# First MLP product as seven half-size block products, the weights' block sums added by GpSimd

## Chip, core and metric

The kernel runs on one core of a Trainium2 chip. The metric is the device time of one execution in microseconds (us). Of a core's engines, TensorE (PE in the profile, PEld for its weight loads) multiplies matrices into PSUM, VectorE (DVE) and ScalarE (ACT) work element by element on SBUF and PSUM, GpSimd (POOL) does so on SBUF, and SyncE (SP) issues the transfers from memory.

## What is computed

A two-layer decoder trunk on 256 tokens of width 2048, all in float32. Each layer is an attention mixer followed by an MLP whose hidden width is 8192; a norm ends it. The change is in the MLP alone:

```python
def sq_relu_mlp(h, w_up, w_down):
    u = jax.nn.relu(h @ w_up)      # (256 x 2048) @ (2048 x 8192)
    return (u * u) @ w_down        # (256 x 8192) @ (8192 x 2048)

# in reference(), for each layer i:
h = h + mixer(rmsnorm(h, norm[i]), ...)
h = h + sq_relu_mlp(rmsnorm(h, mlp_norm[i]), w_up[i], w_down[i])
```

## The kernel before

Tokens are two tiles of 128 (`NT`), the width 2048 is 16 chunks of 128 rows (`KC`), and one PSUM bank holds 512 columns (`HALF`). TensorE multiplies in float32r, so every operand is held as a sum hi + lo of two shorter numbers and a product is made of three: hi·hi, hi·lo and lo·hi. `split` (L172 to L175) makes such a pair: ScalarE casts the source into hi (L174), VectorE subtracts hi from the source into lo (L175). A weight tile of 128 x 1024 is split in one such pair of instructions.

The hidden width is worked through in eight blocks e of 1024 columns. The order in `mlp` (L577) is up(0), up(1) of a block, then the next block's two ups, then `down(e - 1)`; so in the steady part one period is two calls of `up` and one of `down`.

- `up(f)` (L582) makes 512 columns of the first product, transposed. The weights stand still in TensorE and the 256 tokens stream past, hi and lo side by side: for each of 16 chunks and 4 groups of 128 columns, `mm_wide` (L182) issues one product of 512 columns (L185) and one of 256 (L189). `sum_halves` (L193) adds the two halves of a bank, L598 does the squared ReLU, and `split` stores the result, already transposed, as an operand of `down`.
- `down(e)` multiplies that block of 1024 hidden columns by 1024 rows of `w_down`, in two halves of 2 x 512 output columns, by `gemm` (L277): tokens stand still, the weights stream (L296), 8 chunks x 2 token tiles x 3 products x 2 banks, so 192 products of 512 columns. `residual` (L552) adds the result into `h`.

`project` (L557) is the attention's output projection ahead of each MLP; after each half of its columns `norm_transpose` (L210) transposes `h` (L219), applies the gain and splits (L224, L225) into `xm`, the MLP's input.

Weights come by transfers on SP's queue into `wraw`, three buffers of 1 MB; hi tiles (`whi`) have four buffers and lo tiles (`wlo`) three, so the splits run a little ahead of TensorE. PSUM has six banks for accumulators (`ps`) and two for side work (`ps2`, tiles named `side`). The order on each engine is set by a scheduler that works on a list by program order and its own estimates; each engine then runs its list strictly in turn, waiting for semaphores.

Of the kernel before, what the change touches and what calls it, by code (L numbers as in the profile page):

```python
# [17 lines left out]
P = 128  # L18
# [6 lines left out]
NKV = 4  # L25
# [27 lines left out]
ARRIVE = 2  # L53

# [9 lines left out]
def shape_constants():  # L64
    """Rotary tables and position masks; they depend on the shapes alone."""
# [24 lines left out]
def yoco_kernel(ctx: ExitStack, tc: tile.TileContext, x, a_w_in, a_w_out, w_kv, b_w_q, b_w_out, w_up, w_down,  # L90
# [8 lines left out]
    keep = ctx.enter_context(tc.tile_pool(name="keep", bufs=1))  # L99
    wk = ctx.enter_context(tc.tile_pool(name="wk", bufs=2))  # L100
    ps = ctx.enter_context(tc.tile_pool(name="ps", bufs=6, space=bass.MemoryType.PSUM))
    ps2 = ctx.enter_context(tc.tile_pool(name="ps2", bufs=2, space=bass.MemoryType.PSUM))

# [1 line left out]
    def b4(dt=F32):  # L105
        return wk.tile([P, 1024], dt, name="b4" + ("r" if dt == F32R else ""), tag="b4", bufs=4)

    def b3(dt=F32):
        return wk.tile([P, 768], dt, name="b3" + ("r" if dt == F32R else ""), tag="b3", bufs=4)
# [49 lines left out]
    def rope(v, heads, half, tok, idx):  # L159
        """v: [P, heads, hd] view of an SBUF tile, rotated in place."""  # L160
# [21 lines left out]
    def mm_wide(acc, w_hi, w_lo, xk, first, last):  # L182
        """Weights stationary: the first half of acc takes w_hi x_hi + w_lo x_hi, the second w_hi x_lo."""
# [23 lines left out]
    def new_xt():  # L207
        return xtp.tile([P, 4, 2, SEQ], F32R, name="xt")

    def norm_transpose(c4, which):  # L210
        """Chunks 4*c4..4*c4+3 of h, times gain, transposed and split, for each gain in `which`.
        The row's 1/rms is applied where the product comes out."""
# [15 lines left out]

    class Stats:
        """Mean square of the rows of h, and what follows from it."""  # L230
# [34 lines left out]
    def load_w(w, r0, nk, cols, width):  # L265
        """Rows r0.. of nk chunks, `width` columns at each of cols: [P, nk, len(cols) * width]."""
# [36 lines left out]
    def transposed_split(dst, srcs):  # L303
        """dst: [P, hi/lo, n, P] view; srcs: n [P, P] tiles."""
# [7 lines left out]
    # ================= layer 1: sparse attention =================  # L312
# [19 lines left out]
    def arrive(k):  # L332
        """x's next columns, ahead of the product that needs them."""
# [22 lines left out]
    kiT = keep.tile([P, 2, SEQ], F32R, name="kiT")  # L356
    wi = [keep.tile([P, IH], F32, name=f"wi{t}") for t in range(NT)]
    maskA = keep.tile([P, NT, SEQ], F32, name="maskA", tag="layer_mask")
# [3 lines left out]
    def evac_qi(t, s, acc):  # L362
        """Without 1/rms: a positive factor per query, which goes into the heads' weights."""
# [11 lines left out]
    def index_keys():  # L375
        """The indexer's keys and head weights: weights stationary, so the product comes out transposed."""
# [44 lines left out]
    def select(t):  # L421
        """maskA[t]: 0 at the keys that the indexer picks for each query, BIG elsewhere."""
# [38 lines left out]
    kT = keep.tile([P, 2, NKV, SEQ], F32R, name="kT")  # L461
    vv = [keep.tile([P, 2, KV_W], F32R, name=f"vv{t}") for t in range(NT)]
    rkv = []

    def evac_kv(t, s, acc):
        """Keys, rotated and times -SCALE, transposed; values."""
# [14 lines left out]
    def values(kvh, t, n, probs, oT):  # L481
        """probs(r, kb): [P, P] tiles of normalised probabilities of n heads; oT: [P, n, hi/lo, token]."""
# [74 lines left out]
    def project(oTs, w, gains_next, cut):  # L557
        """The first `cut` chunks of both column halves come first: the others' heads may still be at work."""
        st = Stats()
        sets = [[] for _ in gains_next]  # L560
# [3 lines left out]
        flush()  # L564
        for n in range(2):
            gemm(stat, range(cut, KC), w, 0, (n * GW, n * GW + HALF), residual(st, n))
            for c4 in (2 * n, 2 * n + 1):
                for i, xt in enumerate(norm_transpose(c4, gains_next)):
                    sets[i].append(xt)
        return st, sets  # L570

    st, (xm,) = project(oTs, a_w_out[0], [G_M0], CUT_A)

    # ================= squared-ReLU MLP =================
    NE = DFF // GW

    def mlp(i, xm, st_in, gains_next, final=None):  # L577
        """(relu(r * y))^2 = r^2 * relu(y)^2, so the square of 1/rms is applied after the second product."""
# [3 lines left out]
        def up(f):  # L582
            """Columns 512*f.. of the first product, transposed: two halves of a bank, summed on the way out."""
            acc = [ps.tile([P, HALF], F32, name="acc") for _ in range(4)]
            for k4 in range(0, KC, 4):
                raw = load_w(w_up[i], k4 * P, 4, (f * HALF,), HALF)
                for k2 in range(k4, k4 + 4, 2):
                    hi = wp.tile([P, GW], F32R, name="whi", bufs=4).rearrange("p (k c) -> p k c", k=2)
                    lo = wp.tile([P, GW], F32R, name="wlo").rearrange("p (k c) -> p k c", k=2)
                    split(hi, lo, raw[:, k2 - k4:k2 - k4 + 2])  # L590
                    for c in range(4):
                        cs = slice(c * P, (c + 1) * P)
                        for k in (k2, k2 + 1):
                            mm_wide(acc[c], hi[:, k - k2, cs], lo[:, k - k2, cs], xm[k // 4][:, k % 4], k == 0, k == KC - 1)
            ut = new_xt()
            for c in range(4):
                s, q = sum_halves(acc[c]), b1()
                nc.vector.scalar_tensor_tensor(q, s, 0.0, s, op0=ALU.max, op1=ALU.mult)  # L598
                split(ut[:, c, 0], ut[:, c, 1], q)
            us[f] = ut  # L600
# [25 lines left out]
    st, (xkv, xq) = mlp(0, xm, st, [G_KV, G_B])  # L626

# [197 lines left out]
```

## Times and profile before

| what | value |
|---|---|
| median of three runs | 2210.43 us (2209.86 to 2210.74) |
| span of the profiled execution, first to last instruction | 2208.0 us |
| TensorE busy | 2196.8 us, 99% |
| VectorE busy | 1413.6 us, 64% |
| ScalarE busy | 1053.3 us, 48% |
| GpSimd busy | 0.7 us, 6 instructions |
| weights and data moved | 405 MB, mean 184 GB/s |

The profile gives, for one execution, the busy time of each engine, the chain of work that ended last (followed back from the end), groups of instructions by line with their mean duration, and who waited for whom. A busy TensorE is not the same as a TensorE at its peak: products overlap in its pipeline, so the time of a product is best taken from a stretch of products back to back divided by their number. The profiled execution lies 2.4 us below the median of the runs; sums below are made against the 2208.0 us of the span.

### The profile page before, as it was taken

The numbers are of one execution on the slowest core, as the hardware profiler recorded it, in microseconds if no ns is written. First come the engines' busy times: TensorE is split into PE (matmuls) and PEld (weight loads), VectorE is DVE, ScalarE is ACT, GpSimd is POOL, SyncE is SP. The second block draws the span as 40 slices with busy tenths as digits, with TensorE's granted clock in tenths as the row PEclk, the third lists the DMA queues.
The fourth block names the chain that finished last, engine by engine and source line by source line (L and its number), as shares of the span: only waits on it lengthen the run. The fifth ranks groups of instructions, "written<-read, shape, count | busy, mean of one in ns | idle before, by whom it ended". The sixth has DMA issues, their size and how long they took to land.

```text
span 2208.0 us, 29489 instructions
## 1 busy us (share of the span) xinstructions
PE 2196.8 (99%) x11366; PEld 1863.8 (84%) x11366; DVE 1413.6 (64%) x2215; ACT 1053.3 (48%) x1500; POOL 0.7 (0%) x6
## 2 busy tenths in 40 slices
PE   9999999999999999999999999999999999999998
PEld 7788888888888888888888888888888888888886
DVE  5877765656565656567577777666665656565656
ACT  6445554444444434446455555445444434444443
POOL 0000000000000000000000000000000000000000
PEclk9999999999999999999999999999999999999999
DMA  8464456666666666665555454566666665666663
GB/s 305 153 191 136 162 172 191 191 186 193 189 188 193 187 188 192 185 198 180 168 163 164 159 158 150 184 190 191 191 191 191 191 190 191 187 193 190 187 193 138
DMA packets 180749, 405.17 MB, mean 184 GB/s; under 512 B 11008, under 2 KB 60288, under 8 KB 180608
## 3 DMA queue, kind: packets, MB, share of 16 engines
q1 hardware_dynamic: 179456, 401.25, 58.1%
q10 hardware_dynamic: 1152, 2.04, 0.3%
q8 instruction: 89, 1.46, 0.3%
q14 instruction: 52, 0.43, 0.1%
HBM read 401.15 MB, written 2.10 MB: 183 GB/s over the span
## 4 chain that ended last, share of the span: by engine, by line
PE 98%; DVE 1%; ACT 0%; DMA 0%; issue 0%; SPq 0%; DVEq 0%; ACTq 0%
PE acc L296 60%; PE acc L185 22%; PE acc L189 11%; PE side L307 1%; PE side L178 1%; PE side L180 1%; PE side L179 1%; PE side L219 1%; DVE b L439 0%; PE acc L179 0%; PE acc L178 0%; PE acc L180 0%; PE side L660 0%; DMA b<-in_xt_dram 0%; DVE wlo L175 0%; PE side L661 0%
## 5 line engine op out<-in xcount | busy, mean ns | idle before, releaser
L175 DVE TENSOR_TENSOR wlo<-wraw,whi 128x1024 fp32r<-128x1024 f32 (+2 forms) x781 | 919.3, 1177 | 656.8 <-PE acc L296 349.5
L174 ACT CAST whi<-wraw 128x1024 fp32r<-128x1024 f32 (+2 forms) x781 | 792.7, 1015 | 1017.8 <-PE acc L296 610.6
L296 PE MATMUL acc<-whi,xt 128*128 128x512 f32 x4160 | 1093.1, 378 | 0.7 <-ACT whi L174 0.7
L296 PEld LDWEIGHTS acc<-whi,xt 128*128 128x128 f32 x4160 | 741.0, 188 | 140.4 <-ACT whi L174 2.5
L185 PE MATMUL acc<-xt,whi 128*128 128x512 f32 (+1 forms) x2064 | 721.1, 398 | 0.0
L296 PE MATMUL acc<-wlo,xt 128*128 128x512 f32 (+1 forms) x2080 | 616.2, 377 | 0.1
L189 PE MATMUL acc<-xt,wlo 128*128 128x256 f32 (+1 forms) x2064 | 558.5, 281 | 0.0
L185 PEld LDWEIGHTS acc<-xt,whi 128*128 128x128 f32 (+1 forms) x2064 | 379.3, 188 | 84.6
L296 PEld LDWEIGHTS acc<-wlo,xt 128*128 128x128 f32 x2080 | 372.4, 188 | 72.8 <-DVE wlo L175 0.4
L189 PEld LDWEIGHTS acc<-xt,wlo 128*128 128x128 f32 (+1 forms) x2064 | 388.9, 188 | 11.6
L552 DVE SCALAR_TENSOR_TENSOR h<-acc,ri,h 128x512 f32<-128x512 f32 x127 | 88.1, 747 | 11.1 <-PE acc L296 9.2
L174 ACT CAST xt<-b 128x256 fp32r<-128x256 f32 x128 | 51.7, 404 | 31.3 <-DVE b L598 30.3
L196 ACT COPY b<-acc 128x256 f32<-128x256 f32 (+1 forms) x129 | 47.4, 368 | 33.0 <-DVE b L197 31.2
L175 DVE TENSOR_TENSOR xt<-b,xt 128x256 fp32r<-128x256 f32 x128 | 53.9, 421 | 8.5 <-ACT xt L174 8.5
L197 DVE TENSOR_TENSOR b<-acc,b 128x256 f32<-128x256 f32 (+1 forms) x129 | 54.5, 423 | 6.8 <-ACT b L196 3.4
L598 DVE SCALAR_TENSOR_TENSOR b<-b 128x256 f32<-128x256 f32 x128 | 54.0, 422 | 1.7
L307 PE MATMUL side<-ident,b 128*128 128x128 f32 x256 | 38.5, 273 | 0.4 <-DVE b L170 0.4
L307 PEld LDWEIGHTS side<-ident,b 128*128 128x128 f32 x256 | 30.8, 141 | 6.2 <-issue 1.1
L225 DVE SCALAR_TENSOR_TENSOR xt<-side,gT,xt 128x256 fp32r<-128x256 f32 x64 | 28.8, 480 | 7.8 <-ACT xt L224 7.4
L237 ACT ACTIVATE b<-h 128x512 f32<-128x512 f32 (+1 forms) x41 | 25.2, 616 | 17.6 <-DVE h L552 10.6
L224 ACT ACTIVATE xt<-side,gT 128x256 fp32r<-128x256 f32 x64 | 28.3, 473 | 7.4 <-DVE xt L225 4.4
L679 ACT ACTIVATE b<-b,nmb 128x768 f32<-128x768 f32 (+1 forms) x32 | 24.6, 770 | 7.0 <-DVE nmb L676 7.0
(154 smaller groups left out, 750.6 us busy)
## 6 DMA issues: line engine op xcount, KB each, us to landing
wraw<-in_w_up_dram SPq DMA_DIRECT2D x128, 1024.0 KB, 5.7
wraw<-in_w_down_dram SPq DMA_DIRECT2D x128, 1024.0 KB, 5.5
wraw<-in_b_w_q_dram SPq DMA_DIRECT2D x192, 256.0 KB, 3.1
wraw<-in_a_w_in_dram SPq DMA_DIRECT2D x31, 1024.0 KB, 5.3
wraw<-in_a_w_out_dram SPq DMA_DIRECT2D x16, 1024.0 KB, 5.5
wraw<-in_b_w_out_dram SPq DMA_DIRECT2D x16, 1024.0 KB, 5.5
wraw<-in_w_kv_dram SPq DMA_DIRECT2D x8, 1024.0 KB, 4.9
h<-in_x_dram SPq DMA_DIRECT2D x8, 256.0 KB, 8.6
```

The lines of the kernel that those rows point to most:

```text
L174: nc.scalar.copy(hi, src)
L175: nc.vector.tensor_tensor(lo, src, hi.bitcast(F32), op=ALU.subtract)
L185: nc.tensor.matmul(acc, w_hi, xk.rearrange("p a t -> p (a t)"), start=first, stop=last)
L189: nc.tensor.matmul(acc[:, :SEQ], w_lo, xk[:, 0], start=False, stop=False)
L196: nc.scalar.copy(part, acc[:, SEQ:])
L197: nc.vector.tensor_tensor(total, acc[:, :SEQ], part, op=ALU.add)
L224: nc.scalar.activation(xt[:, cc, 0, :], pt[:, j, :], AF.Copy, scale=g)
L225: nc.vector.scalar_tensor_tensor(xt[:, cc, 1, :], pt[:, j, :], g, xt[:, cc, 0, :].bitcast(F32), op0=ALU.mult, op1=ALU.subtract)
L296: nc.tensor.matmul(acc[t][i][:, :c1 - c0], stat(k, a, t), b[:, c0:c1], start=first and a == 0 and b is hi, stop=last and a == 1)
L307: nc.tensor.transpose(pt[:, j * P:(j + 1) * P], sr, ident)
L552: nc.vector.scalar_tensor_tensor(hh, acc, scale()[:, t:t + 1], hh, op0=ALU.mult, op1=ALU.add)
L598: nc.vector.scalar_tensor_tensor(q, s, 0.0, s, op0=ALU.max, op1=ALU.mult)
```

## The change

The first product of the MLP is done for all 1024 columns of a block at once, by Winograd's form of Strassen's scheme: the tokens are halved (two tiles of 128), the reduction is halved into two interleaved sets of chunks, and the 1024 columns are halved into 512 + 512. Seven block products q1 to q7 take the place of eight. Their left operands are seven forms of the normalised activations, made once for each layer; their right operands are the four weight blocks x, w, y, z and three kinds of sums of them. The reduction runs in four steps u; in each, GpSimd makes four sums in place: x + w, then that + y, then that + z, and w + y. Each of the 28 pairs (q, u) is a `task`: a transfer where the block is new, a sum where one is needed, a split, and six products of 512 columns with tokens standing still. `TASKS` sets the order. The seven results are combined by one ScalarE copy and seven VectorE sums; then ReLU and square on ScalarE and a transposition by TensorE, since the result is no longer transposed.

```diff
+BLOCKS = {"x": (0, 0), "w": (0, 1), "y": (1, 1), "z": (1, 0)}
+CHAINS = (("x", None), ("z", None), ("y", None), ("x", "z"), ("x", "w"), ("x", "y"), ("w", "y"))
+NU = 4
+def task_order(gap=3):
+    chains = [c for u in range(NU) for c in ([(0, u), (4, u), (5, u), (3, u)], [(2, u), (6, u)], [(1, u)])]
...
+    open_scope("keep", "att")
...
+    def add_forms(forms, c4, which):
...
+                    nc.scalar.activation(gx[:, cc, :], pt[:, j, :], AF.Copy, scale=g)
...
+        nc.vector.tensor_tensor(s1, a22, a21, op=ALU.subtract)
+        nc.vector.scalar_tensor_tensor(v, s1, -1.0, a11, op0=ALU.mult, op1=ALU.subtract)
+        nc.vector.tensor_tensor(s3, a11, a21, op=ALU.subtract)
+        nc.vector.scalar_tensor_tensor(s4, v, -1.0, a12, op0=ALU.mult, op1=ALU.subtract)
...
+        for f, src in zip(forms, (a11, a12, s4, a22, s1, v, s3)):
+            split(f[:, q, 0], f[:, q, 1], src)
...
+        open_scope("mlp")
+        forms = new_forms()
         for n in range(2):
             gemm(stat, range(cut, KC), w, 0, (n * GW, n * GW + HALF), residual(st, n))
+            add_forms(forms, 2 * n, gain_next)
...
-        def up(f):
-            acc = [ps.tile([P, HALF], F32, name="acc") for _ in range(4)]
...
-                            mm_wide(acc[c], hi[:, k - k2, cs], lo[:, k - k2, cs], xm[k // 4][:, k % 4], k == 0, k == KC - 1)
...
+        def up(e):
+            acc = [ps.tile([P, HALF], F32, name="acc") for _ in range(6)] + [side()]
...
+            def task(q, u):
+                key, other = CHAINS[q]
+                for n in (key, other):
+                    if n is not None and (n, u) not in held:
+                        if n in "xz":
+                            held[n, u] = wx()
+                        else:
+                            both = wp.tile([P, 2, GW], F32, name="wraw", bufs=3)
...
+                            nc.sync.dma_start(held[m, u], block(u, *BLOCKS[m]))
+                if other is not None:
+                    nc.gpsimd.tensor_tensor(held[key, u], held[key, u], held[other, u], op=ALU.add)
...
+                split(hi, lo, held[key, u])
+                for k in range(2):
+                    x = xm[q][:, 2 * u + k]
+                    mm3(acc[q], x[:, 0], x[:, 1], hi[:, k], lo[:, k], u == 0 and k == 0, u == NU - 1 and k == 1)
+            for q, u in TASKS:
+                task(q, u)
+            q1, q2, q3, q4, q5, q6, q7 = acc
+            c11, c12, c21, c22 = (b2() for _ in range(4))
+            nc.scalar.copy(c11, q1)
+            nc.vector.tensor_tensor(c12, q6, c11, op=ALU.add)
...
+                    nc.scalar.activation(c, c, AF.Relu, scale=-1.0 if f else 1.0)
+                    nc.scalar.activation(c, c, AF.Square)
+                    transposed_split(us[2 * e + f][:, :, :, t * P:(t + 1) * P].rearrange("p c a t -> p a c t"),
+                                     [c[:, j * P:(j + 1) * P] for j in range(4)])
...
         for e in range(NE):
-            up(2 * e)
-            up(2 * e + 1)
+            up(e)
             if e:
                 down(e - 1)
```

The blocks x and z have tiles of their own (`wx`, six buffers); w and y share a `wraw` buffer. The tiles of the attention and those of the MLP now lie in the same memory, one set at a time (`open_scope`). The change's line numbers differ from the profile's; in the fences below L685 is GpSimd's sum, L213 the subtraction of a split (L175 before), L631 the residual (L552 before), L698 to L704 the seven sums of results, and L384 the subtraction of a transposed split (L310 before).

GpSimd's list held nothing but the start of the program. In a steady period of the change it holds these rows for one call of `up` (the first eight of sixteen; `wx_3988` and `wx_4000` are block x of steps 0 and 1, `wraw_4012` and `wraw_4036` the pairs w, y of the same steps, `wx_4072` and `wx_4128` block z):

```order
L685 TENSOR_TENSOR wx_3988<-wx_3988,wraw_4012 128x1024
L685 TENSOR_TENSOR wraw_4012<-wraw_4012 128x1024
L685 TENSOR_TENSOR wx_4000<-wx_4000,wraw_4036 128x1024
L685 TENSOR_TENSOR wraw_4036<-wraw_4036 128x1024
L685 TENSOR_TENSOR wx_3988<-wx_3988,wraw_4012 128x1024
L685 TENSOR_TENSOR wx_4000<-wx_4000,wraw_4036 128x1024
L685 TENSOR_TENSOR wx_3988<-wx_3988,wx_4072 128x1024
L685 TENSOR_TENSOR wx_4000<-wx_4000,wx_4128 128x1024
```

All sixteen sums are new; the same tile `wx_3988` is written three times, each time after the split of its former content.

VectorE at the end of a `down` and the start of the next `up`, before:

```order
L175 TENSOR_TENSOR wlo_4003<-wraw_4000,whi_4002 128x1024
L175 TENSOR_TENSOR wlo_4023<-wraw_4000,whi_4022 128x1024
L552 SCALAR_TENSOR_TENSOR h0_2_81<-acc_3852,ri_2882,h0_2_81 128x512
L552 SCALAR_TENSOR_TENSOR h0_3_82<-acc_3853,ri_2882,h0_3_82 128x512
L552 SCALAR_TENSOR_TENSOR h1_2_85<-acc_3854,ri_2882,h1_2_85 128x512
L552 SCALAR_TENSOR_TENSOR h1_3_86<-acc_3855,ri_2882,h1_3_86 128x512
L175 TENSOR_TENSOR wlo_4045<-wraw_4042,whi_4044 128x1024
```

The same place in the change:

```order
L213 TENSOR_TENSOR wlo_3991<-wx_3988,whi_3990 128x1024
L213 TENSOR_TENSOR wlo_4003<-wx_4000,whi_4002 128x1024
L631 SCALAR_TENSOR_TENSOR h0_2_84<-acc_3837,ri_2925,h0_2_84 128x512
L631 SCALAR_TENSOR_TENSOR h0_3_85<-acc_3838,ri_2925,h0_3_85 128x512
L631 SCALAR_TENSOR_TENSOR h1_2_88<-acc_3839,ri_2925,h1_2_88 128x512
L631 SCALAR_TENSOR_TENSOR h1_3_89<-acc_3840,ri_2925,h1_3_89 128x512
L213 TENSOR_TENSOR wlo_4016<-wraw_4012,whi_4015 128x1024
L213 TENSOR_TENSOR wlo_4027<-wx_3988,whi_4026 128x1024
```

Two splits of the coming `up` stand ahead of the four residuals in both; behind them now stand 26 more of that `up` in a row, 16 of which read a tile that GpSimd has just written.

VectorE at the end of an `up`, before (two of the four result tiles of `up`, with splits of `down` between):

```order
L197 TENSOR_TENSOR b1_3693<-acc_3505,b1_3692 128x256
L175 TENSOR_TENSOR wlo_3765<-wraw_3746,whi_3764 128x1024
L598 SCALAR_TENSOR_TENSOR b1_3696<-b1_3693 128x256
L197 TENSOR_TENSOR b1_3701<-acc_3506,b1_3700 128x256
L175 TENSOR_TENSOR xt_3675<-b1_3696,xt_3675 128x256
L598 SCALAR_TENSOR_TENSOR b1_3704<-b1_3701 128x256
```

The same place in the change (`acc_3982` to `acc_3986` and `side_3987` are six of the seven results):

```order
L213 TENSOR_TENSOR wlo_4303<-wraw_4209,whi_4302 128x1024
L213 TENSOR_TENSOR wlo_4369<-wraw_4366,whi_4368 128x1024
L699 TENSOR_TENSOR b2_4312<-acc_3982,b2_4312 128x512
L213 TENSOR_TENSOR wlo_4385<-wraw_4366,whi_4384 128x1024
L700 TENSOR_TENSOR b2_4315<-side_3987,b2_4313 128x512
L213 TENSOR_TENSOR wlo_4403<-wraw_4400,whi_4402 128x1024
L701 TENSOR_TENSOR b2_4313<-acc_3985,b2_4313 128x512
L703 TENSOR_TENSOR b2_4314<-acc_3984,b2_4315 128x512
L702 TENSOR_TENSOR b2_4313<-acc_3983,b2_4313 128x512
L704 TENSOR_TENSOR b2_4315<-acc_3985,b2_4315 128x512
L384 TENSOR_TENSOR xt_4324<-side_4327,xt_4324 128x4x128
L213 TENSOR_TENSOR wlo_4419<-wraw_4400,whi_4418 128x1024
```

The last split of `up` is followed by three of `down`, with the sums of the results between and behind them.

## Rows read from the trace of the kernel before

**Rows 1.** Page: busy time by engine; GpSimd's and the clock's rows by slices.
```profile
PE 2196.8 (99%) x11366; PEld 1863.8 (84%) x11366; DVE 1413.6 (64%) x2215; ACT 1053.3 (48%) x1500; POOL 0.7 (0%) x6
...
POOL 0000000000000000000000000000000000000000
PEclk9999999999999999999999999999999999999999
```

**Rows 2.** Chain in time: start us, length us, what; products of `down`, and transpositions.
```profile
113.93 0.63 PE side L307 x4
...
162.71 0.88 PE side L307 x8
...
411.06 43.52 PE acc L296 x192
499.74 43.52 PE acc L296 x192
...
854.46 43.52 PE acc L296 x192
```

**Rows 3.** Stretches of two `up` and of one `down`: length, busy us by engine, clock.
```profile
core 0: us, PE busy (x) PEld busy (x) DVE busy (x) ACT busy (x) POOL busy (x), PEclk, DMA share, GB/s
454.58:499.74 45.16, 45.16 (x258) 39.19 (x257) 26.36 (x34) 20.56 (x27) 0.00 (x0) 1.00 0.61 184
411.06:454.58 43.52, 43.52 (x193) 36.03 (x193) 26.58 (x32) 18.33 (x21) 0.00 (x0) 1.00 0.63 195
```

**Rows 4.** VectorE in an `up`: start, length, what [idle before, releaser].
```profile
377.29 1.22 DVE L175 TENSOR_TENSOR wlo<-wraw,whi 128x1024 fp32r<-128x1024 f32 x1 [1.58 <-PE acc L189]
380.12 1.23 DVE L175 TENSOR_TENSOR wlo<-wraw,whi 128x1024 fp32r<-128x1024 f32 x1 [1.61 <-PE acc L189]
```

**Rows 5.** Groups by line and shape: count, busy us, mean ns, idle before.
```profile
L175 DVE TENSOR_TENSOR wlo<-wraw,whi 128x1024 fp32r<-128x1024 f32 x649 | 793.9, 1224 | 606.7 <-PE acc L296 314.1 <-PE acc L189 268.4 <-issue 15.6
...
L174 ACT CAST whi<-wraw 128x1024 fp32r<-128x1024 f32 x649 | 683.3, 1053 | 874.7 <-PE acc L296 506.4 <-PE acc L185 325.8 <-issue 33.9
...
L552 DVE SCALAR_TENSOR_TENSOR h<-acc,ri,h 128x512 f32<-128x512 f32 x127 | 88.1, 747 | 11.1 <-PE acc L296 9.2 <-PE acc L180 1.9
...
L175 DVE TENSOR_TENSOR xt<-b,xt 128x256 fp32r<-128x256 f32 x128 | 53.9, 421 | 8.5 <-ACT xt L174 8.5
...
L225 DVE SCALAR_TENSOR_TENSOR xt<-side,gT,xt 128x256 fp32r<-128x256 f32 x64 | 28.8, 480 | 7.8 <-ACT xt L224 7.4
L224 ACT ACTIVATE xt<-side,gT 128x256 fp32r<-128x256 f32 x64 | 28.3, 473 | 7.4 <-DVE xt L225 4.4 <-PE side L219 2.1
L237 ACT ACTIVATE b<-h 128x512 f32<-128x512 f32 x39 | 24.4, 627 | 13.2 <-DVE h L552 10.6 <-DVE h L550 2.4
L550 DVE TENSOR_TENSOR h<-acc,h 128x512 f32<-128x512 f32 x32 | 20.6, 684 | 1.6 <-PE acc L296 1.6
...
L310 DVE TENSOR_TENSOR b4r<-side,b4r 128x512 fp32r<-128x512 f32 x24 | 16.2, 688 | 8.6 <-ACT b4r L309 8.6
...
L309 ACT CAST b4r<-side 128x512 fp32r<-128x512 f32 x24 | 13.6, 585 | 2.6 <-PE side L307 2.6
```

**Rows 6.** The same view, GpSimd alone.
```profile
masks.py:199 POOL TENSOR_SCALAR_AFFINE_SELECT ident<-ident 128x128 f32<-128x128 f32 x1 | 0.3, 292 | 0.1
masks.py:197 POOL MEMSET ident<- 128x128 f32 x1 | 0.2, 204 | 0.3 <-POOLq L813 0.3
...
L813 POOL MEMSET const-float32-0.0<- 128x1 f32 x1 | 0.1, 98 | 0.2 <-issue 0.2
```

**Rows 7.** Transfers: issuer, count, KB each, median us from issue to landing.
```profile
wraw<-in_w_up_dram SPq DMA_DIRECT2D x128, 1024.0 KB, 5.7
```

More of the change, by code (lines that the diff above doesn't have):

```diff
@@ L53 @@
 ARRIVE = 2
+BLOCKS = {"x": (0, 0), "w": (0, 1), "y": (1, 1), "z": (1, 0)}
[3 more added lines that the diff above has]
+    chains = [c for u in range(NU) for c in ([(0, u), (4, u), (5, u), (3, u)], [(2, u), (6, u)], [(1, u)])]
+    place, out = {}, []
+    ahead = 1
+    while any(chains):
+        now = len(out)
+        low = min(c[0][1] for c in chains if c)
+        ready = [c for c in chains if c and c[0][1] <= low + ahead and now - place.get(id(c), -gap) >= gap]
+        if not ready:
+            ready = [c for c in chains if c and c[0][1] <= low + ahead]
+        best = min(ready, key=lambda c: (c[0][1] - len(c), c[0][1]))
+        place[id(best)] = now
+        out.append(best.pop(0))
+    return tuple(out)
+TASKS = task_order()
 Q_W = NH * HD
@@ L98, in yoco_kernel, with open_scope @@
     wp = ctx.enter_context(tc.tile_pool(name="wp", bufs=3))
-    keep = ctx.enter_context(tc.tile_pool(name="keep", bufs=1))
     wk = ctx.enter_context(tc.tile_pool(name="wk", bufs=2))
+    scope = [None]
+    pools = {}
+    def open_scope(*names):
+        if scope[0] is not None:
+            scope[0].close()
+        scope[0] = ExitStack()
+        pools.clear()
+        for n in names:
+            pools[n] = scope[0].enter_context(tc.tile_pool(name=n, bufs=1))
+    open_scope("keep", "att")
     ps = ctx.enter_context(tc.tile_pool(name="ps", bufs=6, space=bass.MemoryType.PSUM))
@@ L354, in yoco_kernel @@
     split_x(0, raw_x)
-    kiT = keep.tile([P, 2, SEQ], F32R, name="kiT")
-    wi = [keep.tile([P, IH], F32, name=f"wi{t}") for t in range(NT)]
-    maskA = keep.tile([P, NT, SEQ], F32, name="maskA", tag="layer_mask")
+    kiT = pools["keep"].tile([P, 2, SEQ], F32R, name="kiT")
+    wi = [pools["keep"].tile([P, IH], F32, name=f"wi{t}") for t in range(NT)]
+    maskA = pools["keep"].tile([P, NT, SEQ], F32, name="maskA", tag="layer_mask")
     qiT = [[None, None] for _ in range(NT)]
@@ L459, in yoco_kernel, with new_kv @@
     enqueue([(index_all(), n_index)], 20)
-    kT = keep.tile([P, 2, NKV, SEQ], F32R, name="kT")
-    vv = [keep.tile([P, 2, KV_W], F32R, name=f"vv{t}") for t in range(NT)]
-    rkv = []
+    kT, vv, rkv = None, [], []
+    def new_kv():
+        nonlocal kT
+        kT = pools["keep"].tile([P, 2, NKV, SEQ], F32R, name="kT")
+        vv[:] = [pools["keep"].tile([P, 2, KV_W], F32R, name=f"vv{t}") for t in range(NT)]
+    new_kv()
     def evac_kv(t, s, acc):
@@ L555, in residual, with project @@
         return evac
-    def project(oTs, w, gains_next, cut):
+    def project(oTs, w, gain_next, cut):
         st = Stats()
-        sets = [[] for _ in gains_next]
         stat = stat_of(oTs)
@@ L564, in project @@
         flush()
+        open_scope("mlp")
+        forms = new_forms()
         for n in range(2):
             gemm(stat, range(cut, KC), w, 0, (n * GW, n * GW + HALF), residual(st, n))
[L567 to L572, printed above, removed]
+            add_forms(forms, 2 * n, gain_next)
+        return st, forms
+    st, xm = project(oTs, a_w_out[0], G_M0, CUT_A)
     NE = DFF // GW
@@ L626, in yoco_kernel @@
     st, (xkv, xq) = mlp(0, xm, st, [G_KV, G_B])
-    mb = keep.tile([P, NG * 3 * P], F32, name="mb", tag="layer_mask")
+    open_scope("keep", "att")
+    new_kv()
+    mb = pools["keep"].tile([P, NG * 3 * P], F32, name="mb", tag="layer_mask")
     nc.scalar.dma_start(mb, c_maskb)
@@ L706, in yoco_kernel @@
             enqueue([(attend_b(kvh, t, qb[t], oTs[-1][:, pr * PAIR:(pr + 1) * PAIR]), steps_b(t)) for t in range(NT)], SPREAD_B)
-    st, (xm,) = project(oTs, b_w_out[0], [G_M1], CUT_B)
-    fg = [b2() for _ in range(4)]
-    for s in range(4):
-        nc.scalar.dma_start(fg[s], final_norm[s * HALF:(s + 1) * HALF].partition_broadcast(P))
+    st, xm = project(oTs, b_w_out[0], G_M1, CUT_B)
     def final(ustat, w, row0, r2):
+        fg = []
+        for _ in range(2):
+            pair = wx()
+            fg += [pair[:, j] for j in range(2)]
+        for s in range(4):
+            nc.scalar.dma_start(fg[s], final_norm[s * HALF:(s + 1) * HALF].partition_broadcast(P))
         st = Stats(5)
```

61 lines of the change are left out of this document (44 added, 17 removed).

## Prediction

> **What bounds the kernel now.** The page first: TensorE is busy for 2196.8 of 2208.0 us at the full granted clock in every slice, and GpSimd does nothing after the first microseconds [rows 1]. Then the chain in time: 192 products of `down` take 43.52 us back to back, and such a stretch begins every 88.68 us (499.74 less 411.06) [rows 2]. So one period, two `up` and one `down`, is 43.52 + 45.16 us, with TensorE busy throughout [rows 3]; there are 16 of them, eight for each layer. VectorE is busy for only 26.4 us of the 45.16 of the two `up`, ScalarE for 20.6 [rows 3]; before each split VectorE idles 1.6 us until TensorE frees a lo tile [rows 4]. TensorE sets the time, and in `up` VectorE and ScalarE have more than 40% to spare. That reserve is what the change draws on.
>
> **TensorE's part.** A product of 512 columns costs 43.52 / 192 = 0.2267 us. In two `up` there are 128 pairs of `mm_wide`, 45.16 / 128 = 0.353 us each. The new `up` has 28 x 6 = 168 products of 512 columns: 168 x 0.2267 = 38.1 us in place of 45.2, 7.1 us less. It adds 16 transpositions at 0.11 to 0.16 us [rows 2], 2.2 us. So TensorE alone would save 4.9 us a period, 78 us in all: 3.5% is the most the change can bring, and any stall over 4.9 us a period eats it.
>
> **Splits and evacuation.** The splits of one block rise from 16 to 28. At 1.224 us on VectorE and 1.053 on ScalarE [rows 5] this is 34.3 and 29.5 us in a stretch of 38.1. VectorE also does the last four residuals of `down`, 4 x 0.747 = 3.0 us, at its start, and one sum of results, 0.68 (like L550), before the last split [rows 5]. So VectorE is at about 95% there. The other six sums (4.1 us) and the four transposed splits (2.75, like L310) [rows 5] fall into `down`, whose 26.6 us of 43.5 [rows 3] have room. ScalarE's eight ReLUs and squares at about 0.63 (like L237) and four casts at 0.585 [rows 5] also do. All this costs nothing while `down`'s splits keep ahead of TensorE; if not, each microsecond counts. At the turn to `down` a bank for its fourth accumulator comes free only after L703, some 5 us after the last product, while TensorE has about 3 us of other work: I count 2 us a period, 0 to 5.
>
> **GpSimd's sums.** Sixteen for each `up`, 128 x 1024 with two operands; no such row exists. Lower bound: VectorE's instruction of that shape, 1.22 us. Nearest row: GpSimd's own select over 128 x 128, 0.292 us [rows 6]; eight times as many elements make 2.34. Its slope (0.292 less 0.098 for one element) makes 1.65 with one operand, twice that, rounded down, 3.2 with two: the upper bound. I take 2.34, the row of the same engine, between the slopes: 16 x 2.34 = 37.4 us, 98% of TensorE's stretch. The Trainium skill, "GPSIMD Engine Reference", § 3, gives 4497 ns for such an add of 2048 elements, so by estimate 2.25 us here; the sum would fall by about 1 us a period.
>
> **Do sum and split run side by side?** This decides. The subtraction of a split reads two operands from SBUF, and so does a sum. In the trace the subtraction keeps one pace, (1224 - 421) / 768 = 1.05 ns an element [rows 5], but with GpSimd idle, so no row shows the two at once. The ends are: side by side, the larger of 34.3 and 37.4; or in turn, their sum, 71.7. I take "in turn", and as a judgement: two engines filled to 95% and 98% have no room for any hindrance, and each block goes back and forth between them (cast, subtract, add, cast, three times over for x), with both lists strictly in order, so that lost time in one is lost in the other. The Trainium skill, "SBUF — State Buffer", § Who interferes with whom, says that a VectorE instruction with two SBUF inputs and a GpSimd instruction that reads SBUF block each other for the whole of an instruction; no run here shows it yet. By that rule the sum is the one that follows, without it that of the first rival.
>
> **The sum, in turn.** Count from the last product of `down`. Its lo tiles free two splits ahead, so (0,0) is split about 4 us earlier, and GpSimd begins. VectorE is then busy with the residuals, whose operands are one in PSUM and one in SBUF, until 3.0 us; GpSimd has finished three sums by then ((4.2 + 3.0) / 2.34). There remain 26 subtractions, 31.8 us, and 13 sums, 30.4: 62.2 in turn. With 3.0 ahead, 0.7 for L698 and 1.3 for the last task's products, `up` takes 67.2 us. `down` takes 43.5 + 2.2 + 2.0 = 47.7. Period 114.9, 26.2 more than 88.7; 16 periods give 419 us. With a sum at 1.22 us (four done ahead): 26 x 1.224 + 12 x 1.224 = 46.5, period 99.2, +168. At 3.2 us (two ahead): 31.8 + 44.8 = 76.6, period 129.3, +650.
>
> **The forms of the activations.** After each half of `project`'s columns VectorE now does four sums and seven subtractions of 512 columns, 11 x 0.69 = 7.6 us, where it did eight of 0.48, 3.8 us; ScalarE does eight copies at 0.47 and seven casts at 0.585 [rows 5], 7.9 us. VectorE's list has all eleven ahead of the next splits, so TensorE runs dry behind the splits already made. Before, the first products of `up` covered this. For layer 1 I count 10 us, for layer 2, where the second part of `project` has only two chunks, 15: 25 us, 10 to 40.
>
> **Counted at nothing.** SP issues 16 transfers of 512 KB in place of 8 of 1 MB for a block; the bytes are the same, the engines' share was 0.61 [rows 3], and a landing takes 5.7 us [rows 7], so six `wx` and three `wraw` buffers cover it; if not, each late block costs up to that. The shared memory of attention and MLP tiles makes the first forms wait for the last head, which `flush` has put ahead of them anyway.
>
> Sum: 2208.0 + 419 + 25 = 2652, and with the 2.4 us by which the median lies above the span, 2655 us.
>
> **Rivals.** *Side by side* (not slower). TensorE stays the bound at 38.1 + 43.5 + 2.2, plus stalls: step (2,0) is split behind the residuals, at 4.2 us against 2.7, 1.5 us; and the 2 us at the turn. Period 87.3, 1.4 less; 16 x 1.4 = 22 saved, 25 lost on the forms: 2213 us. Without these stalls and with the forms at 10 us: 2142. It is faster from the point where stalls and forms together stay below 4.9 us a period. For it: VectorE's pace shows no sign of a limit below 1.05 ns an element. Against it: 95% and 98% of occupation.
> *Partly slowed*: both lengthen each other, but by less than a full turn. Half-way, `up` takes 53 us, the period is 100.4, and the time 2208 + 187 + 25 + 2 = 2422 us.
> *The clock falls as well*: TensorE would be busy for 38 of 67 us in `up`, and the trace has no such stretch; the clock is full in all that I read [rows 1, 3]. At its lower level, 1.2 in place of 2.4 GHz, the products of `up` would take 76 us and bound it: some 9 us a period more, 2800.
>
> **How the numbers follow.** In turn 0.57, in turn with a lower clock 0.05, partly slowed 0.16, side by side 0.22. The predicted time is that of "in turn". Its own range is 2400 to 2890 by the bounds of a sum; "partly slowed" reaches from 2240 to 2400 and over, "side by side" from 2142 to 2240, about half of it above 2200. From 2200 to 2800 leaves out some 0.11 below and 0.07 above. A measurement of this kernel tells 0.2%, 4.4 us, from no change. Faster by more than that takes side by side with few stalls: 0.13. Within it: 0.05. Slower: 0.82.
>
> **What the profile would show.** In turn: in `up` TensorE waits at nearly every task for the hi or lo tile; GpSimd's and VectorE's busy times add to about the length of the stretch, or L213 and L685 read longer than 1.22 and 2.3 us because the waiting lies inside the instruction; `down` still takes about 44 us. Side by side: L213 stays at 1.224 beside a running sum, TensorE stays at 97% or more, `up` near 40 us. The forms: a gap of TensorE of some 10 us ahead of each MLP. The prediction would be wrong if sums took 1.2 us or less, or if the two engines read SBUF without hindering each other; and the price of the forms would be wrong if the first tasks of `up` need fewer of them than VectorE's list suggests.

## The result and the profile after

The changed kernel takes 2609.03 us, the median of four runs (2608.41 to 2610.23), against 2210.59 us before in the same comparison: a ratio of 1.180, 95% interval 1.1786 to 1.182. Slower, by 398 us. The forecast of 2655 us is 46 us too high; the range of 2200 to 2800 holds it.

The page of the changed kernel, its busy times and three of its rows by slices:

```profile
PE 2245.3 (86%) x10214; PEld 1787.2 (69%) x10214; DVE 2012.2 (77%) x2211; ACT 1274.1 (49%) x1672; POOL 785.6 (30%) x262
...
PE   9999967968879697889999999957968778697888
...
POOL 0000077163351724520000000076163452725420
...
PEclk9999989999999999999999999988999999999999
```

TensorE, busy for 99% of the span before [rows 1], now has slices at 5 to 8 tenths, and they are those in which GpSimd works. Its clock stays near full. The same page's chain of work that ended last, by engine; GpSimd and VectorE now hold 27% of it:

```profile
PE 63%; POOL 19%; DVE 8%; issue 7%; ACT 2%; DMA 1%; POOLq 0%; DVEq 0%; ACTq 0%
```

The chain in time (start, length, what) gives the period, as [rows 2] did:

```profile
480.32 34.27 PE acc L370 x151
591.00 34.27 PE acc L370 x151
```

591.00 less 480.32 is 110.68 us, where it was 88.68: 22.0 more, and 352 us in 16 periods. Stretches of one `up` and of the `down` behind it (columns as in [rows 3]):

```profile
517.59:582.20 64.61, 44.45 (x169) 32.04 (x168) 60.11 (x33) 28.73 (x29) 44.80 (x15) 0.95 0.36 114
582.20:628.27 46.07, 45.91 (x210) 37.33 (x208) 30.22 (x32) 23.09 (x28) 4.26 (x2) 1.00 0.62 206
```

`down` keeps TensorE busy for 45.91 of 46.07 us. In `up` TensorE stands still for 20 of 64.6 us, while VectorE is on record as busy for 60 and GpSimd for 45 of them. The groups by line and shape tell what that busy time is:

```profile
L213 DVE TENSOR_TENSOR wlo<-wx,whi 128x1024 fp32r<-128x1024 f32 x320 | 678.4, 2148 | 105.0 <-ACT whi L212 67.1 <-PE acc L370 35.9
...
L685 POOL TENSOR_TENSOR wx<-wx,wraw 128x1024 f32<-128x1024 f32 x128 | 384.6, 3010 | 1596.1 <-DVE wlo L213 1593.6 <-ACT b L708 2.5
```

The subtraction of a split, 1224 ns on average before [rows 5], has a mean of 2148 ns on the tiles that GpSimd also works on, with the same shape and types. The timeline of VectorE at the start and in the middle of an `up` (start, length, what, idle before):

```profile
516.65 2.71 DVE L631 SCALAR_TENSOR_TENSOR h<-acc,ri,h 128x512 f32<-128x512 f32 x4
...
522.35 4.54 DVE L213 TENSOR_TENSOR wlo<-wx,whi 128x1024 fp32r<-128x1024 f32 x2
526.81 3.41 DVE L213 TENSOR_TENSOR wlo<-wraw,whi 128x1024 fp32r<-128x1024 f32 x1
530.25 12.36 DVE L213 TENSOR_TENSOR wlo<-wx,whi 128x1024 fp32r<-128x1024 f32 x5
542.53 1.21 DVE L213 TENSOR_TENSOR wlo<-wraw,whi 128x1024 fp32r<-128x1024 f32 x1
543.67 6.73 DVE L213 TENSOR_TENSOR wlo<-wx,whi 128x1024 fp32r<-128x1024 f32 x2
```

and that of GpSimd in the same `up`:

```profile
515.73 3.27 POOL L685 TENSOR_TENSOR wraw<-wraw 128x1024 f32<-128x1024 f32 x1
...
525.83 6.63 POOL L685 TENSOR_TENSOR wx<-wx,wraw 128x1024 f32<-128x1024 f32 x2 [1.16 <-DVE wlo L213]
...
572.95 2.39 POOL L685 TENSOR_TENSOR wx<-wx 128x1024 f32<-128x1024 f32 x1 [4.61 <-DVE wlo L213]
```

The chain of waits through this place, in time:

```profile
525.83 3.32 POOL wx L685
529.17 1.05 ACT whi L212
530.25 3.31 DVE wlo L213
533.63 3.31 POOL wx L685
536.93 1.12 issue
538.10 3.42 POOL wx L685
```

Read them together. The sum that starts at 525.83 takes 3.32 us, so it ends at 529.15. The subtraction that starts at 526.81 ends at 530.22, 1.07 us behind the sum's end: it waited 2.3 us and then did its own work. The sum in its turn began while the subtraction before it was still running, until 526.89 (the pair from 522.35), and needed 2.3 us from there. Each instruction is on record as running from its start, so the wait lies inside its length: 3.4 us for either, where a sum undisturbed takes 2.39 us (the row at 572.95) and a subtraction 1.21 (542.53). Where subtractions follow each other undisturbed, the next starts 1.14 us after the last (543.67 less 542.53). The four residuals at 516.65 run beside a sum, the one from 515.73 to 519.00, and are not held up: 2.71 us for four, and 742 ns as the mean of L631 in the whole run, where it was 747 before [rows 5]. They have one 128x512 operand in SBUF and one in PSUM. So it is not any work of VectorE that waits, but the subtraction with both operands in SBUF.

The last view is of the start of layer 1's MLP, where the forms of the activations are made; rows of TensorE's timeline, and the stretch of the first 18 products of `up`, 328.94 to 338.84:

```profile
328.94 0.79 PE L216 MATMUL acc<-whi,xf 128*128 128x512 f32 x1 [5.06 <-ACT whi L212]
331.35 0.79 PE L216 MATMUL acc<-whi,xf 128*128 128x512 f32 x1 [1.62 <-ACT whi L212]
332.69 0.80 PE L217 MATMUL acc<-wlo,xf 128*128 128x512 f32 x1 [0.54 <-DVE wlo L213]
...
338.84 0.40 PE L216 MATMUL acc<-whi,xt 128*128 128x512 f32 x1
...
328.94:338.84 9.90, 7.73 (x19) 5.46 (x19) 6.54 (x9) 3.41 (x4) 5.90 (x2) 0.55 0.30 99
```

TensorE waits 5.06 us for the first split of `up` and 1.62 and 0.54 us for the next ones, and the granted clock of these 9.90 us is 0.55, near the lower of its two levels.

### The profile page after: what moved, and what is told of

It is laid out like the page before. It is cut to its first block, busy times and chain, and to the rows that moved or that the text cites. A ratio compares the mean times of both kernels' runs of the same rounds, so it can differ in the third digit from the quotient of the medians.

```text
span 2607.4 us, 28432 instructions
## 1 busy us (share of the span) xinstructions
PE 2245.3 (86%) x10214; PEld 1787.2 (69%) x10214; DVE 2012.2 (77%) x2211; ACT 1274.1 (49%) x1672; POOL 785.6 (30%) x262
## 4 chain that ended last, share of the span: by engine, by line
PE 63%; POOL 19%; DVE 8%; issue 7%; ACT 2%; DMA 1%; POOLq 0%; DVEq 0%; ACTq 0%
PE acc L370 49%; POOL wx L685 15%; DVE wlo L213 6%; POOL wraw L685 4%; PE acc L217 2%; PE side L381 2%; PE acc L218 2%; PE acc L216 2%; ACT whi L212 1%; PE side L216 1%; PE side L217 1%; PE side L218 1%; DVE h L631 1%; ACT wx L291 0%; DMA wraw<-in_w_up_dram 0%
## 5 line engine op out<-in xcount | busy, mean ns | idle before, releaser
L213 DVE TENSOR_TENSOR wlo<-wraw,whi 128x1024 fp32r<-128x1024 f32 (+2 forms) x653 | 873.0, 1339 | 353.0 <-PE acc L370 271.6
L370 PE MATMUL acc<-whi,xt 128*128 128x512 f32 x4160 | 1102.6, 380 | 0.0
L212 ACT CAST whi<-wraw 128x1024 fp32r<-128x1024 f32 (+2 forms) x653 | 657.0, 1007 | 632.8 <-PE acc L370 510.4
L685 POOL TENSOR_TENSOR wx<-wx,wraw 128x1024 f32<-128x1024 f32 x128 | 384.6, 3010 | 1596.1 <-DVE wlo L213 1593.6
L213 DVE TENSOR_TENSOR wlo<-wx,whi 128x1024 fp32r<-128x1024 f32 x320 | 678.4, 2148 | 105.0 <-ACT whi L212 67.1
L212 ACT CAST whi<-wx 128x1024 fp32r<-128x1024 f32 x320 | 328.6, 1045 | 595.1 <-POOL wx L685 505.1
L217 PE MATMUL acc<-wlo,xt 128*128 128x512 f32 x392 | 176.8, 451 | 175.3 <-DVE wlo L213 175.2
L217 PE MATMUL acc<-wlo,xf 128*128 128x512 f32 x384 | 161.9, 422 | 91.6 <-DVE wlo L213 91.6
L685 POOL TENSOR_TENSOR wx<-wx 128x1024 f32<-128x1024 f32 x64 | 199.4, 3116 | 115.0 <-DVE wlo L213 108.9
L685 POOL TENSOR_TENSOR wraw<-wraw 128x1024 f32<-128x1024 f32 x64 | 202.9, 3171 | 5.0
L216 PE MATMUL acc<-whi,xt 128*128 128x512 f32 x392 | 163.6, 417 | 33.8 <-ACT whi L212 33.8
L216 PE MATMUL acc<-whi,xf 128*128 128x512 f32 x384 | 156.5, 408 | 13.4 <-ACT whi L212 13.4
L218 PE MATMUL acc<-whi,xt 128*128 128x512 f32 x392 | 163.6, 417 | 0.0
L218 PE MATMUL acc<-whi,xf 128*128 128x512 f32 x384 | 153.8, 401 | 0.0
L631 DVE SCALAR_TENSOR_TENSOR h<-acc,ri,h 128x512 f32<-128x512 f32 x127 | 87.4, 742 | 7.5 <-PE acc L370 5.5
```

The source lines that it names most:

```text
L216: nc.tensor.matmul(o, a_hi, b_hi, start=start, stop=False)
L217: nc.tensor.matmul(o, a_hi, b_lo, start=False, stop=False)
L218: nc.tensor.matmul(o, a_lo, b_hi, start=False, stop=stop)
L370: nc.tensor.matmul(acc[t][i][:, :c1 - c0], stat(k, a, t), b[:, c0:c1], start=first and a == 0 and b is hi, stop=last and a == 1)
L631: nc.vector.scalar_tensor_tensor(hh, acc, scale()[:, t:t + 1], hh, op0=ALU.mult, op1=ALU.add)
L685: nc.gpsimd.tensor_tensor(held[key, u], held[key, u], held[other, u], op=ALU.add)
```

## Experiments

The theory: a sum on GpSimd and a subtraction on VectorE, both with two operands in SBUF, take turns at reading. Its rivals: the sums merely take too long for a stretch of 38 us; or the round of cast, subtraction and sum is held up by its order alone; or it is not the reading but any work of GpSimd that holds VectorE up. The kernels with the sums on VectorE and as transfers were run four times each, the others once; the kernel before took 2210.3 to 2210.4 us beside them.

**Without the sums.** The sums are left out, so the splits work on unsummed blocks:

```
-                if other is not None:
-                    nc.gpsimd.tensor_tensor(held[key, u], held[key, u], held[other, u], op=ALU.add)
```

> The change with GpSimd's sums left out (the products then take unsummed blocks; all transfers, splits and products stay). Theory, sum and subtraction take turns: an up falls from 64.6 us to TensorE's 38.1 plus some 2 us of waiting at its start, a period to about 86 us, the run to 2607 - 16 x 24 = 2220 us (2200 to 2250), with the subtraction at 1.22 us everywhere. What then stands over 2208 - 16 x 2.7 is the price of the forms, some 45 us by the profile of the change. Rival, that ScalarE and VectorE alone cannot feed TensorE with 28 splits in 38 us: up stays above 45 us and the run above 2300.

Measured: 2176.43 us. Groups of this kernel, and the stretch of one whole period:

```profile
L213 DVE TENSOR_TENSOR wlo<-wx,whi 128x1024 fp32r<-128x1024 f32 x320 | 388.5, 1224 | 70.6 <-PE acc L370 35.9 <-PE acc L217 20.4 <-ACT whi L212 1.1
...
507.09:591.41 84.32, 84.32 (x377) 69.13 (x377) 64.96 (x64) 52.94 (x58) 0.00 (x0) 1.00 0.62 200
```

The subtraction is back at 1224 ns, and TensorE is busy for all of an 84.32 us period. So the whole loss comes with the sums. The time lies below the range that was expected, since the period is 84.3 us and not some 86. VectorE carries the 28 subtractions, the residuals and the combination without delay, and the 2 us that the prediction set aside for the turn to `down` are not there.

**Without the subtractions.** In `up` the hi tile is cast and used for the lo tile as well; the sums stay:

```
-                lo = wp.tile([P, GW], F32R, name="wlo").rearrange("p (k c) -> p k c", k=2)
-                split(hi, lo, held[key, u])
+                nc.scalar.copy(hi, held[key, u])
...
-                    mm3(acc[q], x[:, 0], x[:, 1], hi[:, k], lo[:, k], u == 0 and k == 0, u == NU - 1 and k == 1)
+                    mm3(acc[q], x[:, 0], x[:, 1], hi[:, k], hi[:, k], u == 0 and k == 0, u == NU - 1 and k == 1)
```

> The change with the subtractions of up's splits left out (the products take hi in place of lo); GpSimd's sums, with both operands, stay. Theory of turns: with no subtraction beside it a sum takes 2.2 to 2.4 us throughout instead of 3.1 on the mean, 16 x 2.3 = 37 us fit beside TensorE's 38, up falls to about 41 us and the run to 2220 to 2260 us. Rival, that GpSimd itself needs 3.1 us for a sum and its chain of sums, casts and waits bounds up: the mean stays at 3.0 us or more, up at 52 us or more, the run above 2400.

Measured: 2202.64 us. GpSimd's group, and the stretch of one `up`:

```profile
L685 POOL TENSOR_TENSOR wx<-wx,wraw 128x1024 f32<-128x1024 f32 x128 | 310.4, 2436 | 1439.3 <-ACT whi L687 1439.3
...
468.80:507.90 39.10, 39.08 (x169) 31.39 (x168) 4.52 (x7) 28.25 (x29) 31.27 (x14) 1.00 0.56 172
```

A sum takes 2.44 us where it took 3.01, and the sixteen of them, with the casts between, fit: the `up` in the second row takes 39.1 us, with TensorE busy throughout. It was expected at 41, so the time lies below the expected range. Either of the two engines alone fits; only both together do not. That rules out that the sums alone are too long. Order alone is not ruled out by this: with the subtractions a link of the round is gone too. The lengths that shrink do rule it out, since a wait for order would stand in the idle time, not in the instruction.

**GpSimd that only writes.** Each sum is replaced by two fills of the same tile with a constant; they wait for the releases of that tile, though not for the second block, and hold up the same casts:

```
-                    nc.gpsimd.tensor_tensor(held[key, u], held[key, u], held[other, u], op=ALU.add)
+                    for _ in range(2):
+                        nc.gpsimd.memset(held[key, u], 0.01)
```

> Each sum replaced by two memsets of the same tile on GpSimd, which write as much twice over and read nothing (the sums are left out; some 0.9 us each by the memset row of the kernel before). Theory, it is the reading that excludes: the subtraction stays at 1.22 us beside them, up at about 41 us, the run at 2220 to 2260 us. Rival, any GpSimd access to SBUF excludes VectorE's subtraction: subtractions of 2 us and more appear, up takes 28 x 1.2 + 32 x 0.9 + 5 = 68 us less the head start, the run lies above 2450.

Measured: 2187.10 us. Groups:

```profile
L213 DVE TENSOR_TENSOR wlo<-wx,whi 128x1024 fp32r<-128x1024 f32 x320 | 381.7, 1222 | 111.1 <-ACT whi L212 68.6 <-PE acc L370 35.9 <-PE acc L218 4.8
...
L686 POOL MEMSET wx<- 128x1024 f32 x384 | 363.9, 956 | 238.4 <-DVE wlo L213 229.3
```

GpSimd is at work for 1.9 us in each place of a sum, in the same order between casts and splits, and the subtraction does not feel it: 1222 ns. The rival "any work of GpSimd" falls, and so does "order alone", at least for links of 1.9 us. What holds VectorE up comes with GpSimd's reading and not with its writing. The run is faster than expected, since `up` takes some 39 us and not 41.

**GpSimd that reads one operand.** The sum becomes a multiplication by a constant, in place; the second block is not added:

```
-                    nc.gpsimd.tensor_tensor(held[key, u], held[key, u], held[other, u], op=ALU.add)
+                    nc.gpsimd.tensor_scalar(held[key, u], held[key, u], 1.25, None, op0=ALU.mult)
```

> Each sum replaced by a multiplication of the same tile by a constant on GpSimd: one operand read from SBUF in place of two (the sums are left out). Theory of turns, if one read is enough to block: the own time falls to about 1.65 us by the slope of GpSimd's select, some subtractions still read 1.2 + 1.6 = 2.8 us, up falls by about 16 x 0.6 = 10 us and the run to some 2450 us. If one operand leaves room for the subtraction's two: the subtraction stays at 1.22 us, up at 41 us, the run near 2240.

Measured: 2392.55 us, near neither. GpSimd's and VectorE's groups, then rows of the timelines of the two: GpSimd's before the first `up` and in a later one, and VectorE's in that one:

```profile
L685 POOL TENSOR_SCALAR wx<-wx 128x1024 f32<-128x1024 f32 x192 | 594.7, 3111 | 158.2 <-DVE wlo L213 156.3
L213 DVE TENSOR_TENSOR wlo<-wx,whi 128x1024 fp32r<-128x1024 f32 x320 | 429.5, 1359 | 230.2 <-ACT whi L212 173.7 <-PE acc L370 32.1 <-PE acc L218 24.2
...
316.06 2.77 POOL L685 TENSOR_SCALAR wraw<-wraw 128x1024 f32<-128x1024 f32 x1 [8.96 <-DMA wraw<-in_w_up_dram]
595.71 9.00 POOL L685 TENSOR_SCALAR wx<-wx 128x1024 f32<-128x1024 f32 x3 [0.56 <-DVE wlo L213]
604.68 2.76 POOL L685 TENSOR_SCALAR wraw<-wraw 128x1024 f32<-128x1024 f32 x1
...
602.71 1.34 DVE L213 TENSOR_TENSOR wlo<-wx,whi 128x1024 fp32r<-128x1024 f32 x1 [0.64 <-ACT whi L212]
```

Two assumptions of the expectation were wrong. The multiplication is not short: it takes 2.77 us (the one at 316.06) where VectorE does nothing beside it, longer than the sum of two operands, so this is its own length and no wait. And it does not shut the subtraction out: the one at 602.71 lies wholly inside GpSimd's work from 595.71 to 604.68 and takes 1.34 us; the mean is 1359 ns against 2148 in the change. What this kernel loses it loses to GpSimd's own length, 16 x 3.1 = 49 us in an `up`, for which the casts wait. The longest subtraction of a split in this run takes 2.09 us, so some are held up, but for no more than 0.9 us. So a one-operand read disturbs the subtraction a little, a two-operand read for its whole length. Why the one-operand instruction is longer, and what it shares with VectorE for how long, stays open.

**Half-size sums.** The sums cover 512 of the 1024 columns of a tile:

```
-                    nc.gpsimd.tensor_tensor(held[key, u], held[key, u], held[other, u], op=ALU.add)
+                    hc = slice(0, HALF // 2)
+                    nc.gpsimd.tensor_tensor(held[key, u][:, :, hc], held[key, u][:, :, hc], held[other, u][:, :, hc], op=ALU.add)
```

> Sums over half the columns only (128 x 512 in place of 128 x 1024; the other half is left unsummed), everything else as in the change. Theory of turns: a sum's own time halves, 2.2 to about 1.2 us, and as each microsecond of it is one of up, up falls by 16 x 1.0 = 16 us to some 48 us, the run to 2607 - 16 x 16 = 2350 us (2320 to 2400). Rival, fixed cost of each handover between the engines: up falls by less than 8 us and the run stays above 2480. Rival, side by side with GpSimd as the bound: up falls to TensorE's 40 us, the run to 2230.

Measured: 2342.69 us. The subtraction's group:

```profile
L213 DVE TENSOR_TENSOR wlo<-wx,whi 128x1024 fp32r<-128x1024 f32 x320 | 524.3, 1666 | 84.2 <-ACT whi L212 43.9 <-PE acc L370 35.9 <-PE acc L218 2.3
```

As expected, it lies between no sums and whole ones, 2176 and 2609, and so does the subtraction, 1666 ns between 1224 and 2148. The loss grows with the amount that GpSimd reads, though not in proportion: 166 us for the first half and 266 for the second. It tells no theories apart that the runs above had not.

**The sums on VectorE.** Nothing is left out; one engine name changes:

```
-                    nc.gpsimd.tensor_tensor(held[key, u], held[key, u], held[other, u], op=ALU.add)
+                    nc.vector.tensor_tensor(held[key, u], held[key, u], held[other, u], op=ALU.add)
```

> The sums moved from GpSimd to VectorE, nothing left out. Theory of turns: a sum costs the pair 2.2 us on GpSimd but 1.22 on VectorE, so up falls to 44 x 1.21 + 3.0 + 0.7 + 1.3 = 58 us less two subtractions done ahead, some 56 us, a period to 102 us, the run to 2607 - 16 x 8.5 = 2470 us (2430 to 2510), although the busier engine now does all of it. Rival, that the two engines gain anything from running at once: the move to one engine makes it slower than 2607.

Measured, four runs: 2387.5 us (2384.6 to 2390.8), 1.081 of the kernel before (1.0789 to 1.0825). The sums' group and the stretch of one period:

```profile
L685 DVE TENSOR_TENSOR wx<-wx,wraw 128x1024 f32<-128x1024 f32 x128 | 153.5, 1221 | 0.5
...
452.09:548.45 96.36, 89.21 (x377) 68.62 (x377) 81.67 (x80) 51.13 (x58) 0.00 (x0) 1.00 0.55 175
```

This is the plainest evidence that two engines in turn are not two engines: with all sums on VectorE and GpSimd idle, the kernel is 221 us faster than with the work "shared", since a sum takes 1.14 to 1.22 us there and 2.35 on GpSimd. The expectation was 82 us too high, some 5 us a period. It counted each instruction at its recorded length, and 44 x 0.07 makes 3 us of this; and it had no sum done ahead of the residuals, where the trace of this period has two (at 484.30 and 485.56, the residuals at 487.83). `up` now takes about 50.3 us (96.36 less the 46.07 of `down` in the change).

**The sums as transfers.** Each sum is a transfer from SBUF to SBUF that accumulates at its destination, issued on GpSimd's queue; nothing is left out:

```
-                    nc.gpsimd.tensor_tensor(held[key, u], held[key, u], held[other, u], op=ALU.add)
+                    nc.gpsimd.dma_start(held[key, u], held[other, u], accum_op=ALU.add)
```

> The sums made by transfers that add into their destination, SBUF to SBUF, issued from GpSimd's queue, nothing left out. Theory of turns: no engine reads both operands, the subtraction stays at 1.22 us, and only the latency of a transfer, 3 to 4.5 us from issue to landing as for other 512 KB transfers, lengthens the chain cast, subtract, sum: 1.05 + 1.22 + 4 = 6.3 us a link against 3 tasks of 1.36. With three links for each of four blocks x, staggered, up takes 45 to 60 us and the run 2280 to 2520 us; near 2220 if the order hides the latency. Rival, GpSimd's issue or the 16 transfer engines bind (share 0.6 before, half as many bytes more): above 2600.

Measured, four runs: 2685.47 us, 1.216 of the kernel before (1.2138 to 1.2174). From the view of transfers, from that of waits (total us, times, longest), and the stretch of one `up` (the last columns are clock, share of the transfer engines' time, GB/s):

```profile
wx<-wraw POOLq DMA_DIRECT2D x128, 512.0 KB, 6.8
...
ACT whi L212 <- DMA wx<-wraw: 406.2, 114, 8.4
...
ACT whi L212 <- DMA wx<-wx: 186.4, 44, 7.9
...
526.10:597.30 71.20, 51.34 (x174) 36.09 (x173) 35.95 (x34) 29.49 (x32) 12.06 (x14) 0.88 0.94 221
```

The subtraction keeps 1223 ns here, so nothing takes turns. But the time is 165 us above the expected range and where the rival put it, above 2600: an `up` takes 71.2 us. A transfer needs 6.8 us from issue to landing, not 4, x needs three sums one behind the other, and the casts wait for them. The transfer engines are busy for 0.94 of that `up`, 0.36 in the change, so the rival that they bind is not ruled out: whether the latency or the load of the engines sets the time, and how far the load makes the latency, was not told apart.

**Without making the forms.** The transpositions, sums and splits of the activations ahead of each MLP are left out; the tiles are filled with a constant on GpSimd while it is idle:

```
-        g2 = []
-        for c in (c4, c4 + 1):
...
-            split(f[:, q, 0], f[:, q, 1], src)
+        for f in forms:
+            nc.gpsimd.memset(f[:, q].bitcast(F32), 0.01)
```

> The change with the seven forms of the activations left out: they are filled with a constant by GpSimd while it is idle, so that the transpositions, sums and splits of add_forms go, and all else stays. Theory: the forms cost what lies between TensorE's last product of project and the first of up, 10 us a layer in the trace, and the products run at the lower clock after it: 40 to 50 us in all, the run at 2557 to 2570 us. By the prediction's count of 25 us: 2582.

Measured: 2564.86 us, as expected, and 44 us below the change. Rows of its timeline and of its chain that answer to those at 328.94, 338.84 and 480.32 of the change, and the stretch of its first 18 products:

```profile
317.21 0.40 PE L216 MATMUL acc<-whi,xf 128*128 128x512 f32 x1
...
321.41 0.40 PE L216 MATMUL acc<-whi,xt 128*128 128x512 f32 x1
...
317.21:321.41 4.20, 4.20 (x19) 3.38 (x18) 4.20 (x5) 2.06 (x5) 4.20 (x2) 1.00 0.00 0
...
460.02 34.27 PE acc L350 x151
```

The first product of layer 1's `up` comes 11.7 us earlier, the nineteenth 17.4 us, and by the first steady `down` the lead is 20.3 us. So over half of the price falls before the first product, and most of the rest in the first 18 products: they take 9.9 us in the change, at a clock of 0.55 and with waits of 1.62 and 0.54 us for their splits, and 4.2 us here, at full clock and without a wait, since the splits had run ahead. Of these 5.7 us the two waits are 2.2, and the rest goes with the lower clock. In layer 2 the first product, in the change and here, is at

```profile
1702.33 0.80 PE L216 MATMUL acc<-whi,xf 128*128 128x512 f32 x1 [5.06 <-ACT whi L212]
...
1664.56 0.40 PE L216 MATMUL acc<-whi,xf 128*128 128x512 f32 x1
```

The lead is 37.8 us there, 20.4 of them brought from layer 1, so 17.4 fall before the first product; the spans differ by 44.3 us at the end, so some 7 come behind it.

## The prediction, point by point

**Do sum and split run side by side: right.** "In turn" was a judgement without a row, and the runs show it: subtraction alone 1224 ns, sum alone 2.35 to 2.44 us, together up to 3.4 for either, with the wait inside. The main marks named for it are there: TensorE waits in `up` at task after task, L213 and L685 read longer, `down` keeps its time. The Trainium skill, "SBUF — State Buffer", § Who interferes with whom, has it that a VectorE instruction with two SBUF inputs and a GpSimd instruction that reads SBUF block each other, and one that only writes does not. The sums (2148 ns for a subtraction) and the fills (1222 ns) agree; the one-operand multiplication does not (1359 ns, and at most 2.09 us beside an instruction of 2.77), and there the measurement decides.

**GpSimd's sum: right.** 2.34 us was taken from a row of 128 x 128 at eight times the elements; the undisturbed one takes 2.35 to 2.39. That is luck in part: the row was of another instruction with one operand, and the one-operand multiplication takes 2.77.

**The sum of an `up`: 2.6 us too high.** 67.2 against 64.6. The term that was mis-sized is mainly the subtraction's: 26 at 1.224, the recorded length, where back to back they follow at 1.14; 26 x 0.08 = 2.1 us by this count. Recorded lengths overlap a little at their ends, and [rows 4] could not show it, since before each subtraction VectorE idled.

**The turn to `down`: 2 us that were mostly not needed.** 46.1 against 47.7, of which 43.5 + 2.2 are products and transpositions. TensorE is busy for 45.91 us of the 46.07: the transpositions and the first products of `down` fill the time until L703 frees the fourth bank. Together the period is 110.7 against 114.9, and 16 x 4.2 = 67 us is what the forecast was over.

**The forms: 44 us, not 25.** Here the forecast was under by 19 us. The step that failed counted only what comes before the first product of `up`. It had 10 us there in layer 1 and 15 in layer 2, where the runs show 11.7 and 17.4: near enough. But the price goes on behind the first product, in an `up` that starts with no splits ahead and at a clock of 0.55. There it is 8.6 us in layer 1 and some 7 in layer 2, put at nothing, which makes 20.3 and 24. The upper bound given, 40, was too low. The clock stood among the rivals as a matter of `up` as a whole, and it is 0.95 in a steady one; what counted was its fall in the first products behind a pause.

**The account.** 2208.0 + 352 + 44 = 2604, against a span of 2607.4. The forecast came within 46 us partly because its two errors, 67 over and 19 under, have opposite signs. The kernel without the forms leaves out the transposing and splitting of the activations as well, which the kernel before also had, so 44 is rather an upper end for what the change added there; 3 us or somewhat more have no place in the account.

**TensorE's part: right, and small.** 38.1 + 43.5 + 2.2 = 83.8 us a period was forecast with nothing in the way, and without the sums it is 84.32. So Strassen's scheme would give 4.4 us a period, 70 us in all, of which the forms and what hangs on them take half: 34 us is what is left when the sums cost nothing. That is the *side by side* rival with its better end, at 2176 between its 2142 and 2213. *Partly slowed*, at 2422, did not come about with the sums: each waits out the other's reading. The prediction's 95% for VectorE in `up` was low: its own terms, 34.3 + 3.0 + 0.68, fill 38.0 of 38.1 us, 35.5 with two splits done ahead; it did no harm, as the run without the sums shows.

**A better version?** None of those tried that keep the sums beats the kernel before. The nearest, sums on VectorE, has VectorE busy for 81.67 us of a period against TensorE's 84.3 without the sums; spread evenly over `up` and `down` it would be at 97% with no slack for the order, and could gain at most the 34 us. That was not tried.

## What to carry to other kernels

An idle engine is only free work if it shares nothing with the busy one beside it: before moving work to it, ask which operands both read from SBUF at the same time, and add the two times where each reads two, as the sums and subtractions do here. In a trace, look for such a conflict in the lengths of instructions that did not change, not in idle time, for there it does not show. And price what is done once ahead of a stage by what covers it there and by how the first products of the stage behind it start, not by its instructions alone.

## What was not expected of the hardware

- A one-operand multiplication of 128 x 1024 on GpSimd takes 2.77 us undisturbed, longer than the sum of two operands of that shape, 2.35 to 2.39; with it the subtraction on VectorE takes 1.36 us on average, not 2.15.
- Subtractions of 128 x 1024 on VectorE start every 1.14 us when back to back, though each is on record with 1.21.
- An accumulating transfer of 512 KB from SBUF to SBUF lands after 6.8 us by the median, in a run whose transfer engines are busy for 0.94 of an `up`, and costs GpSimd 0.9 us to issue:

```profile
L685 POOL DMA_DIRECT2D wx<-wraw x128 | 115.7, 906 | 1814.0 <-DVE wlo L213 1227.3 <-DMA wx<-in_w_up_dram 578.3 <-issue 4.5
```
